# Two mixer layers on one core: the q, k, z and gm projections by Strassen's product, ahead of values and attention

## The chip, the core and the metric

The kernel runs on one core of one Trainium2 chip. The metric is the device time of one execution in microseconds (us). The kernel before took 2031.75 us, the median of 3 runs (2031.7 to 2031.75). Beside it stands the profile of one execution, taken by the hardware profiler. Its engines are PE (TensorE matmul), PEld (TensorE weight load), DVE (VectorE), ACT (ScalarE), POOL (GpSimd) and SP (SyncE, which here only issues DMAs).

## The reference, cut to what matters

Two layers run over 512 latent and 256 context tokens of 1024 features. Each layer normalises its input, projects it by one large matrix, runs two token mixers of 8 heads each (retention and mLSTM, forwards and backwards), and merges them under gates:

```
h  = rmsnorm(x) * (1 + scale) + shift                     # 768 tokens x 1024
u  = h @ w_in + b_in                                       # 1024 -> 11 * 1024 + 32
rq, rk, rv, rz, mq, mk, mv, mo, mz, mg, gr, gm = split(u)  # 1024 each, mg 32
mq, mk = silu(dwconv5(mq, mk)) ; rq, rk = rope(rq, rk) on latent tokens
rx = retention(rq, rk, rv) ; mx = mlstm(mq, mk, mv, mg)    # chunks of 128 tokens, both directions
yr = headnorm(rx) * silu(rz) ; ym = headnorm(sigmoid(mo) * mx) * silu(mz)
y  = sigmoid(gr) * (yr @ w_ret_o) + sigmoid(gm) * (ym @ w_ml_o)
x  = x + gate * (y @ w_out)
```

In the last layer only the latent tokens of the output are wanted, so context tokens need k and v alone there (`need` is false). The matrices are float32 and the result is held to float32.

## The kernel before, in words

Activations lie transposed: features on the 128 partitions, tokens on the free axis, the 256 context tokens first. h is kept as two tiles of 8 feature blocks, a float32r part (hi) and its remainder (lo). Every weight block (1024 x 128, 512 KB) is loaded from DRAM and split in the same way: `split` lets ACT write the float32r part and DVE write `raw - hi` (L161, L162). A projection of one block of 128 output features (`proj`, L208) is 8 feature blocks times three products (hi*hi, hi*lo, lo*hi): 24 matmuls over the 512 latent tokens (L216) and, where context is wanted, 24 over the 256 context tokens (L218), all summed in PSUM. Values are projected with tokens on the partitions (`projv`, L232, 256 columns a matmul).

There are 56 such blocks of q, k, z and gm in a layer: rq, rk, rz, mq, mk, mz and gm, 8 blocks each. In layer 0 all 56 need context; in layer 1 only the 16 of rk and mk do. Their results are used at once and stay on chip: rotary for rq and rk (`rope`: DVE reads the PSUM result three times, POOL adds, L651 to L654), the 5-tap convolution for mq and mk (`ml_qk`: ACT copies PSUM to u, DVE makes six passes over 770 or 512 columns, L789 to L797), silu for rz and mz (`gate_z`), and a tanh for gm, which alone goes to DRAM and comes back at the merge.

The order of the work: generators stand for the attention of a head (`ret_att`, `ml_att`) and for side work; after every projection `tick()` advances each of them by one stage, so that the matmuls of the next heads' projections stand between the attention matmuls of a head. Side work is the computation of the later modulation vectors (`ada_rest`, 32 blocks: 14 scalar_tensor_tensor passes of 128 columns and a few small ones on DVE for each block, L354 to L356; 12 blocks run in layer 0's retention stage, 20 from the gm stage on) and the mLSTM gates. A scheduler then settles each engine's instruction order. Buffers: two weight slots (`wh`, `wl`), three raw slots, six stage tiles, five large tiles of 24 KB a partition (tags b0 to b4; b0 and b1 hold h, b2 to b4 the attention's workspace).

## Time and profile before

| of the profiled execution | |
|---|---|
| span, first to last instruction | 2032.1 us (the page gives no other time of it; the runs' median is 2031.75) |
| PE busy | 1990.1 us (98%), 12676 matmuls |
| PEld busy | 1799.9 us (89%) |
| DVE busy | 1427.0 us (70%), 3303 instructions |
| ACT busy | 718.9 us (35%) |
| POOL busy | 370.0 us (18%), 431 instructions |
| granted TensorE clock, mean | 0.993 of 2.4 GHz |
| DMA | 229.59 MB, 113 GB/s |

How to read it: an engine's busy time is the time in which at least one of its instructions is under way, waiting for operands' ports included. One instruction's duration reaches some way into the next one's, so a row of instructions takes less than the sum of their durations. A stretch's limit is read from the stretch, not from these shares.

### The profile page before, as it was taken

The page shows a single profiled execution, that of the slowest core. Times are in us where ns is not written, and L with a number is a line of the kernel's source. Part 1 is how long each engine was busy: PE and PEld are TensorE (multiplying, and loading weights), DVE is VectorE, ACT ScalarE, POOL GpSimd, SP SyncE. Part 2 cuts the span into 40 slices and gives each one's busy share as a digit, 9 for nine tenths or more (in the row PEclk, how much of TensorE's full clock was granted, in tenths as well). Part 3 has the DMA queues.
Part 4 walks back from the last instruction along what each step waited for, and adds up shares of the span by engine and source line. Part 5 has one row for each costly group of instructions (what it writes and reads, how often), then busy time and mean ns, then how long its engine had stood idle before and what let it go on. Part 6 is the DMA issues. An engine that isn't in the chain of part 4 may idle for free.

```text
span 2032.1 us, 32593 instructions
## 1 busy us (share of the span) xinstructions
PE 1990.1 (98%) x12676; PEld 1799.9 (89%) x12676; DVE 1427.0 (70%) x3303; ACT 718.9 (35%) x1362; POOL 370.0 (18%) x431
## 2 busy tenths in 40 slices
PE   6989999999999999999999999999999999999997
PEld 6988989999999999888888888899899999988887
DVE  7886996566858585888834689655667886763356
ACT  5423222334434434343212442322334444434223
POOL 4312222221212121100000341312212122110000
PEclk9999999999999999999999999999999999999999
DMA  8213322212322323454524431222233333325435
GB/s 297 75 45 104 123 81 84 71 57 101 106 82 88 100 85 98 162 175 153 175 86 158 152 101 45 96 71 76 76 112 103 117 120 121 114 98 184 137 120 171
DMA packets 74716, 229.59 MB, mean 113 GB/s; under 512 B 8960, under 2 KB 17408, under 8 KB 73536
## 3 DMA queue, kind: packets, MB, share of 16 engines
q1 hardware_dynamic: 70464, 211.56, 32.0%
q0 software_dynamic: 4096, 15.93, 2.0%
q8 instruction: 100, 1.64, 0.3%
q14 instruction: 56, 0.46, 0.1%
HBM read 206.29 MB, written 21.17 MB: 112 GB/s over the span
## 4 chain that ended last, share of the span: by engine, by line
PE 87%; DVE 9%; issue 2%; DMA 1%; ACT 0%; POOL 0%; SPq 0%; POOLq 0%; DVEq 0%; ACTq 0%
PE mv L232 11%; PE mqk_l L216 9%; PE rqk_l L216 7%; PE bm_l L216 4%; PE gm_l L216 4%; PE br_l L216 4%; PE mz_l L216 4%; PE gr_l L216 4%; PE rv L232 4%; PE ou L205 4%; PE mqk_c L218 3%; PE rz_l L216 3%; PE rqk_c L218 2%; PE ro L743 2%; PE mo L869 2%
## 5 line engine op out<-in xcount | busy, mean ns | idle before, releaser
L232 PE MATMUL mv<-wh_vo,h_hi 128*128 128x256 f32 x640 | 183.6, 287 | 0.0
L232 PE MATMUL mv<-wl_vo,h_hi 128*128 128x256 f32 x640 | 183.2, 286 | 0.0
L232 PE MATMUL mv<-wh_vo,h_lo 128*128 128x256 f32 x640 | 182.0, 284 | 0.0
L356 DVE SCALAR_TENSOR_TENSOR aacc<-gw,sil,aacc 128x128 f32<-128x128 f32 x448 | 138.7, 362 | 0.0
L232 PEld LDWEIGHTS mv<-wh_vo,h_hi 128*128 128x128 f32 x640 | 122.6, 191 | 0.4
L232 PEld LDWEIGHTS mv<-wh_vo,h_lo 128*128 128x128 f32 x640 | 122.5, 191 | 0.2
L792 DVE SCALAR_TENSOR_TENSOR cv<-u,vec,cv 128x770 f32<-128x770 f32 (+1 forms) x128 | 121.3, 949 | 1.8
L232 PEld LDWEIGHTS mv<-wl_vo,h_hi 128*128 128x128 f32 x640 | 122.4, 191 | 0.0
L822 POOL TENSOR_TENSOR ws<-ws,gw 128x768 f32<-128x768 f32 (+1 forms) x32 | 53.3, 1686 | 321.5 <-PE mo L871 155.1
L216 PE MATMUL mqk_l<-h_lo,wh_mqk 128*128 128x512 f32 x256 | 103.8, 405 | 0.0
L216 PE MATMUL mqk_l<-h_hi,wh_mqk 128*128 128x512 f32 x256 | 103.3, 403 | 0.0
L216 PE MATMUL mqk_l<-h_hi,wl_mqk 128*128 128x512 f32 x256 | 102.4, 400 | 0.0
L654 POOL TENSOR_TENSOR ws<-ws,rp 128x512 f32<-128x512 f32 x32 | 52.6, 1644 | 189.6 <-DVE ws L653 149.6
L232 PE MATMUL rv<-wl_rv,h_hi 128*128 128x256 f32 x288 | 83.2, 289 | 0.0
L232 PE MATMUL rv<-wh_rv,h_hi 128*128 128x256 f32 x288 | 83.1, 289 | 0.0
L232 PE MATMUL rv<-wh_rv,h_lo 128*128 128x256 f32 x288 | 82.8, 288 | 0.0
L205 PE MATMUL ou<-yl,wh_wout 128*128 128x256 f32 (+1 forms) x256 | 79.1, 310 | 0.0
L205 PE MATMUL ou<-yh,wl_wout 128*128 128x256 f32 (+1 forms) x256 | 79.1, 310 | 0.0
L205 PE MATMUL ou<-yh,wh_wout 128*128 128x256 f32 (+1 forms) x256 | 78.7, 309 | 0.0
L743 PE MATMUL ro<-ws,ws 128*128 128x128 f32 x448 | 65.2, 279 | 9.5 <-DVE gsm L563 3.9
L695 POOL TENSOR_TENSOR ws<-ws,ws 128x768 f32<-128x768 f32 (+1 forms) x32 | 53.1, 1678 | 106.4 <-PE ro L743 106.2
L743 PEld LDWEIGHTS ro<-ws,ws 128*128 128x128 f32 x448 | 59.7, 194 | 12.8 <-DVE st L744 8.1
(444 smaller groups left out, 6536.2 us busy)
## 6 DMA issues: line engine op xcount, KB each, us to landing
gw<-in_wada SPq DMA_DIRECT2D x32, 512.0 KB, 3.4
raw_vo<-in_wblk SPq DMA_DIRECT2D x32, 512.0 KB, 4.2
raw_mqk<-in_wblk SPq DMA_DIRECT2D x32, 512.0 KB, 3.8
raw_wout<-in_wout SPq DMA_DIRECT2D x32, 512.0 KB, 3.9
gw<-grow SPq DMA_DIRECT2D x8, 1536.0 KB, 6.3
raw_qk<-in_wblk SPq DMA_DIRECT2D x16, 512.0 KB, 3.4
raw_zq<-in_wblk SPq DMA_DIRECT2D x16, 512.0 KB, 3.3
...
```

The lines of the kernel that those rows point to most:

```text
L205: pe.matmul(dst, lw[:, j, kb], mv[:, kb, sl], start=first, stop=last)
L216: pe.matmul(lat, lw[:, j, kb], mv[:, kb, LAT], start=first, stop=last)
L218: pe.matmul(c[:, :NCTX], lw[:, j, kb], mv[:, kb, CTX], start=first, stop=last)
L232: pe.matmul(dst, sx[:, kb, tk], mv[:, :, kb], start=first, stop=last)
L356: v.scalar_tensor_tensor(o, raw[:, kb], sil[:, kb, d:d + 1], o, op0=OP.mult, op1=OP.add)
L654: g.tensor_tensor(dst[:, LAT], dst[:, LAT], t[:, :512], op=OP.add)
L695: g.tensor_tensor(chunks(qd[d][:, qsl], nq), chunks(qT[:, qsl], nq), xi[d][:, None, :].to_broadcast([P, nq, P]), op=OP.mult)
L743: pe.matmul(o, lt, rt, start=k == 0, stop=k == len(ops) - 1)
L792: v.scalar_tensor_tensor(y[:, o0:o0 + n], u[:, o0 + i:o0 + i + n], cw[i], y[:, o0:o0 + n], op0=OP.mult, op1=OP.add)
L822: g.tensor_tensor(qd[d][:, qsl], qT[:, qsl], gw[:, 2 + d, qsl], op=OP.mult)
L869: pe.matmul(o, ch(sT[d], n), vt[:, n, 0:129], start=True, stop=first)
```

## The change: what it does

At the start of each layer, before any value or attention, all 56 blocks of q, k, z and gm are projected. The first four gm blocks are computed as before (`plain`). The other 52 go two at a time through Strassen's product in Winograd's form (`strassen`): the weight pair is a 2 x 2 grid of parts (two output blocks by two halves of the features), h is a 2 x 2 grid (two halves of the features by two halves of the tokens, 384 tokens each, or 256 where only latent tokens are wanted). Seven products of 12 matmuls (`product`, L684: 4 feature blocks times the three hi/lo products, 384 or 256 columns) stand in place of the eight of a plain block product.

The sums that this needs are new work. Of h, four combinations T1 to T4 are made once a layer (`make_forms`: POOL adds hi and lo, DVE makes the differences, then `split`). Of each weight pair POOL makes four sums or differences of 512 columns (`prep`, L652 to L660), and seven forms are split by ACT and DVE, 512 columns each, where two blocks of 1024 were split before. Of the products, ACT copies three partial sums out of PSUM and DVE adds three PSUM results to them (`out`, L694); `done` then does the rotary, convolution, silu or tanh from SBUF, and writes each block to DRAM from POOL's queue. Twelve blocks of `ada_rest` are ticked into this phase in layer 0. The tokens of h are stored in a permuted order, weights go through four single slots w0 to w3 and four quarter-size raw tags.

Then comes `rvg` and, in place of the old mixed loop, value projections with the attention of the heads; q, k and z of a head are fetched from DRAM two or three heads ahead (`fetch_qk`, `fetch_z`). gr is computed after the attention, its first half through DRAM. The merge and output stages are as before.

On DVE, in layer 0 before the change, the convolution of mLSTM head 0 stands between the statistics of retention head 7 and the split of the next weights (`cv` convolution, `st`, `mvs` statistics, `wl_vo` weights):

```order
L789 TENSOR_SCALAR cv_0_0_4142<-u_0_0_4141,vec_98 128x770
L792 SCALAR_TENSOR_TENSOR cv_0_0_4142<-u_0_0_4141,vec_98,cv_0_0_4142 128x770 x4
L795 SCALAR_TENSOR_TENSOR ws_0_470<-u_0_0_4141,cv_0_0_4142 128x512
L797 SCALAR_TENSOR_TENSOR ws_0_470<-u_0_0_4141,cv_0_0_4142 128x256
L744 BN_STATS st_7_4272<-ro_7_0_4273 128x6
L162 TENSOR_TENSOR wl_vo_0_4314<-raw_vo_0_0_4315,wh_vo_0_4313 128x1024
L745 BN_AGGR mvs_7_4271<-st_7_4272 128x2
L744 BN_STATS st_7_4272<-ro_7_2_4282 128x6
L162 TENSOR_TENSOR wl_vo_0_4314<-raw_vo_0_1_4319,wh_vo_0_4313 128x1024
L745 BN_AGGR mvs_7_4271<-st_7_4272 128x2
```

After the change, in the phase ahead of the attention (`w_st_11` forms of weight pair 11, `cv_mk` and `cv_mq` convolutions of two different pairs, `aacc` modulation vectors, `ub` the results; pairs count from 0):

```order
L175 TENSOR_TENSOR w_st_11_2692<-raw_st_11_01_2667,w_st_11_2692 128x512
L379 TENSOR_SCALAR aacc_12_2630<-gw_474,sil 128x128
L556 TENSOR_SCALAR cv_mk_2760<-ub_824,vec_98 128x770
L379 TENSOR_SCALAR aacc_12_2630<-gw_474,sil 128x128
L175 TENSOR_TENSOR w_st_11_2769<-raw_st_11_10_2553,w_st_11_2769 128x512
L175 TENSOR_TENSOR w_st_11_2769<-raw_st_11_11_2555,w_st_11_2769 128x512
L562 SCALAR_TENSOR_TENSOR cv_mq_2489<-ub_824,cv_mq_2489 128x770
L381 SCALAR_TENSOR_TENSOR aacc_12_2630<-gw_474,sil,aacc_12_2630 128x128
L175 TENSOR_TENSOR ahl_12_2627<-aacc_12_2417,ahl_12_2627 128x256
L559 SCALAR_TENSOR_TENSOR cv_mk_2760<-ub_824,vec_98,cv_mk_2760 128x770
L540 SCALAR_TENSOR_TENSOR ub_824<-rzt_2_2660,ub_824 128x768
```

The convolution, the silu of a z pair and the modulation vectors now stand among the splits of the weight forms, several pairs' work at once; no attention work is there.

On POOL, in the retention stage of layer 0 before (`rp` rotary adds, `ve_r` the norm's power, `yrd` results to DRAM, L695 the decayed queries):

```order
L623 TENSOR_TENSOR ve_r_3_2699<-ve_r_3_2699,nhalf 128x6
L654 TENSOR_TENSOR ws_0_470<-ws_0_470,rp_5_0_2912 128x512
L636 DMA yrd_3_480<-yo_r_3_2918 128x768
L654 TENSOR_TENSOR ws_0_470<-ws_0_470,rp_5_1_3037 128x512
L695 TENSOR_TENSOR ws_0_472<-ws_0_470,ws_0_472 128x768 x2
L623 TENSOR_TENSOR ve_r_4_3141<-ve_r_4_3141,nhalf 128x6
L675 TENSOR_TENSOR ws_0_472<-rt_5_3282 128x128
L636 DMA yrd_4_481<-yo_r_4_3270 128x768
L654 TENSOR_TENSOR ws_0_470<-ws_0_470,rp_6_0_3444 128x512
L654 TENSOR_TENSOR ws_0_470<-ws_0_470,rp_6_1_3500 128x512
```

After the change, in the new phase (`raw_st` weight sums in place, `ub` with L652 and L655 the two shared sums, `mkd`, `rkd`, `mzd` results to DRAM):

```order
L652 TENSOR_TENSOR ub_824<-raw_st_8_10_2071,raw_st_8_11_2073 128x512
L563 DMA mkd_1_527<-cv_mk_1808 128x770
L656 TENSOR_TENSOR raw_st_8_10_2071<-raw_st_8_00_2069,raw_st_8_10_2071 128x512
L563 DMA mkd_0_526<-cv_mk_1849 128x770
L549 TENSOR_TENSOR ub_824<-ub_824,rp_rk_1951 128x2x256
L550 DMA rkd_1_503<-ub_824 128x768
L660 TENSOR_TENSOR raw_st_7_01_2025<-raw_st_7_01_2025,ub_824 128x512
L655 TENSOR_TENSOR ub_824<-ub_824,raw_st_8_00_2069 128x512
L652 TENSOR_TENSOR ub_824<-raw_st_9_10_2237,raw_st_9_11_2239 128x512
L541 DMA mzd_1_535<-ub_824 128x768
L656 TENSOR_TENSOR raw_st_9_10_2237<-raw_st_9_00_2235,raw_st_9_10_2237 128x512
```

Four 512-column adds for each pair of weight blocks and the rotary adds stand in one row with the DMA issues of the results, which each wait for DVE's last pass over that result.

The diff, cut to its core:

```diff
+            def done(kind, j, u, n):
+
+                dst = st[kind][j]
...
+                elif kind in ("rz", "mz"):
+                    t = stage(f"{kind}t{l}_{j}")
+                    s.activation(t[:, :2 * n], u[:, :2 * n], AF.Tanh, scale=0.5)
+                    v.scalar_tensor_tensor(u[:, :2 * n], t[:, :2 * n], 1.0, u[:, :2 * n], op0=OP.add, op1=OP.mult)
+                    g.dma_start(dst[:, :2 * n], u[:, :2 * n])
+                elif kind in ("rq", "rk"):
...
+                    v.tensor_tensor(tv[0:64], ul[64:128], sv[64:128], op=OP.mult)
+                    v.tensor_tensor(tv[64:128], ul[0:64], sv[0:64], op=OP.mult)
+                    v.tensor_tensor(ul, ul, nat2(cosT), op=OP.mult)
+                    g.tensor_tensor(ul, ul, tv, op=OP.add)
+                    g.dma_start(dst[:, :2 * n], u[:, :2 * n])
...
+                    cw = [vc[:, V_CW + blk * 5 + i:V_CW + blk * 5 + i + 1] for i in range(5)]
+                    v.tensor_scalar(y[:, o0:o0 + m], u[:, o0:o0 + m], cw[0], vc[:, V_CB + blk:V_CB + blk + 1],
+                                    op0=OP.mult, op1=OP.add)
+                    for i in range(1, 5):
+                        v.scalar_tensor_tensor(y[:, o0:o0 + m], u[:, o0 + i:o0 + i + m], cw[i], y[:, o0:o0 + m],
+                                               op0=OP.mult, op1=OP.add)
+                    s.activation(u[:, o0:o0 + m], y[:, o0:o0 + m], AF.Tanh, scale=0.5)
+                    v.scalar_tensor_tensor(y[:, o0:o0 + m], u[:, o0:o0 + m], 1.0, y[:, o0:o0 + m], op0=OP.add, op1=OP.mult)
+                    g.dma_start(dst[:, o0:o0 + m], y[:, o0:o0 + m])
...
+            def make_forms(sl):
+                n = 256 if sl is LAT else P
+                c0 = P if sl is LAT else 0
+                for k in range(4):
+                    t0, t1 = stage(f"fa{l}_{k}_{n}"), stage(f"fb{l}_{k}_{n}")
+                    for t, kb in ((t0, k), (t1, k + 4)):
+                        g.tensor_tensor(nat2(t[:, :2 * n]), hv2(hp[0][:, kb].bitcast(F32), sl), hv2(hp[1][:, kb].bitcast(F32), sl),
+                                        op=OP.add)
+                    (a0, b0_), (a1, b1_) = [(t[:, 0:n], t[:, n:2 * n]) for t in (t0, t1)]
+                    f12, f34 = stage(f"fc{l}_{k}_{n}"), stage(f"fd{l}_{k}_{n}")
+                    v.tensor_tensor(f12[:, 0:n], b0_, a0, op=OP.subtract)
+                    v.tensor_tensor(f12[:, n:2 * n], b1_, f12[:, 0:n], op=OP.subtract)
+                    v.tensor_tensor(f34[:, 0:n], b1_, b0_, op=OP.subtract)
+                    v.tensor_tensor(f34[:, n:2 * n], a1, f12[:, n:2 * n], op=OP.subtract)
+                    for f, tf in ((f12, t12), (f34, t34)):
+                        split(tf[:, 0, :, k, c0:c0 + n], tf[:, 1, :, k, c0:c0 + n], nat2(f[:, :2 * n]))
...
+            def strassen(pairs):
+
...
+                def prep(i, k):
+                    if i >= nu:
+                        return
+                    w = wslot(k, f"st{l}_{i}")[:, :2 * KB * P].rearrange("p (f h c) -> p f h c", f=2, h=2)
+                    W[i, k] = w
+                    r = R[i]
+
+                    def form(f, a):
+                        split(w[:, f, 0], w[:, f, 1], a)
+                    if k == 0:
+                        g.tensor_tensor(s1b, r[1, 0], r[1, 1], op=OP.add)
+                        form(0, r[0, 0])
+                        form(1, s1b)
+                        g.tensor_tensor(s2b, s1b, r[0, 0], op=OP.subtract)
+                        g.tensor_tensor(r[1, 0], r[0, 0], r[1, 0], op=OP.subtract)
+                    elif k == 1:
+                        form(0, s2b)
+                        form(1, r[0, 1])
+                        g.tensor_tensor(r[0, 1], r[0, 1], s2b, op=OP.subtract)
+                    elif k == 2:
+                        form(0, r[1, 0])
+                        form(1, r[1, 1])
+                    else:
+                        form(0, r[0, 1])
...
+                def product(i, ps, k, f, form, first, last):
+                    n = pairs[i][2]
+                    w = W[i, k]
+                    for kk in range(4):
+                        xh, xl = act(form, kk, n)
+                        for hl, x in ((0, xh), (0, xl), (1, xh)):
+                            pe.matmul(ps[:, :n], w[:, f, hl, kk * P:(kk + 1) * P], x, start=first and kk == 0 and hl == 0 and x is xh,
+                                      stop=kk == 3 and hl == 1, skip_group_check=True)
+
+                def out(i, o, half, ps, add=None):
+                    kind, j0, n = pairs[i]
+                    b = vc[:, VB[kind] + j0 + o:VB[kind] + j0 + o + 1]
+                    for dst, c in pieces(kind, U[i][o], half, n):
+                        if add is None:
+                            s.activation(dst, ps[:, c], AF.Identity, bias=b)
+                        else:
+                            v.scalar_tensor_tensor(dst, ps[:, c], b, add[:, c], op0=OP.add, op1=OP.add)
...
+                three = (("ra", 0, 0), ("rb", 1, 0), ("rc", 1, 1))
+                raws_of(0, three + (("rd", 0, 1),))
+                prep(0, 0)
+                prep(0, 1)
+                yield
+                for i, (kind, j0, n) in enumerate(pairs):
+                    U[i] = [ub[:, 774 * (2 * (i % 2) + o):774 * (2 * (i % 2) + o + 1)] for o in range(2)]
+                    u2s = ub[:, 3864 + 384 * (i % 2):4248 + 384 * (i % 2)]
+                    if kind in ("mq", "mk"):
+                        for u in U[i]:
+                            pads(u, n)
+                    raws_of(i + 1, three)
+                    X[i], Z[i] = atile("lat", f"sx{l}_{i}"), atile("ctx", f"sz{l}_{i}")
+                    product(i, X[i], 0, 0, "B11", True, False)
+                    s.activation(p1s[:, :n], X[i][:, :n], AF.Copy)
+                    product(i, Z[i], 0, 1, "T1", True, False)
+                    yield
+                    p4(i - 1)
+                    prep(i, 2)
+                    product(i, X[i], 1, 0, "T2", False, False)
+                    s.activation(u2s[:, :n], X[i][:, :n], AF.Copy)
+                    yield
+                    p3(i - 1)
+                    prep(i, 3)
+                    raws_of(i + 1, (("rd", 0, 1),))
+                    prep(i + 1, 0)
+                    Y = btile(f"sy{l}_{i}")
+                    product(i, Y, 1, 1, "B21", True, True)
+                    out(i, 0, 0, Y, p1s)
+                    prep(i + 1, 1)
+                    product(i, X[i], 2, 0, "T3", False, False)
+                    s.activation(u3s[:, :n], X[i][:, :n], AF.Copy)
+                    out(i, 1, 1, Z[i], u3s)
+                    yield
+                p4(nu - 1)
+                wload(wpos[0])
+                p3(nu - 1)
...
+            first = plain(0, True)
+            next(first)
+            t12 = big.tile([P, 2, 2, 4, 384], F32R, tag="b3", name=f"t12_{l}")
+            t34 = big.tile([P, 2, 2, 4, 384], F32R, tag="b4", name=f"t34_{l}")
+            make_forms(LAT)
+            for _ in first:
+                pass
+            ub = big.tile([P, 6144], F32, tag="b2", name=f"ub{l}")
+            todo = [("gm", 4, need), ("gm", 6, need)]
+            for j in (0, 2, 4, 6):
+                todo += [("mq", j, need), ("rz", j, need), ("mk", j, True), ("rk", j, True), ("mz", j, need), ("rq", j, need)]
+            run = strassen([(k, j, 384 if full else 256) for k, j, full in todo])
+            for _ in plain(2, False):
+                make_forms(CTX)
+                next(run)
+            if l == 0:
+                ada_todo = [(0, b) for b in range(16, 24)] + [(1, b) for b in range(24)]
+                side.append(ada_rest(gw, ada_todo[:ADAN]))
+            for i, _ in enumerate(run):
+                if i % 4 == 3:
+                    tick()
+            drain(side)
+
 
```

## Rows read from the trace of the kernel before

**Rows 1.** Stretches: length, sum, busy PE, PEld, DVE, ACT, POOL; PEclk, DMA share, GB/s.

```profile
100.00:150.00 50.00, 44.25 (x284) 40.87 (x283) 45.24 (x95) 10.92 (x18) 7.36 (x7) 0.93 0.14 45
220.00:310.00 90.00, 89.41 (x607) 81.93 (x606) 89.36 (x279) 28.27 (x59) 19.79 (x14) 1.00 0.30 99
570.00:675.00 105.00, 105.00 (x744) 98.12 (x743) 77.51 (x196) 42.21 (x94) 20.39 (x30) 1.00 0.29 93
```

**Rows 2.** The chain that ended last, by engine, from the page.

```profile
PE 87%; DVE 9%; issue 2%; DMA 1%; ACT 0%; POOL 0%; SPq 0%; POOLq 0%; DVEq 0%; ACTq 0%
```

**Rows 3.** Timeline of PE, three places: start us, duration us, what.

```profile
700.10 0.40 PE L216 MATMUL mqk_l<-h_hi,wh_mqk 128*128 128x512 f32 x1
...
700.45 0.40 PE L216 MATMUL mqk_l<-h_lo,wh_mqk 128*128 128x512 f32 x1
...
707.94 0.28 PE L232 MATMUL mv<-wh_vo,h_lo 128*128 128x256 f32 x1
708.06 0.28 PE L232 MATMUL mv<-wl_vo,h_hi 128*128 128x256 f32 x1
...
1850.12 0.39 PE L216 MATMUL gr_l<-h_lo,wh_gr 128*128 128x512 f32 x1
1850.35 0.39 PE L216 MATMUL gr_l<-h_hi,wl_gr 128*128 128x512 f32 x1
```

**Rows 4.** DVE groups by line and shape: busy us, mean ns, idle before.

```profile
L356 DVE SCALAR_TENSOR_TENSOR aacc<-gw,sil,aacc 128x128 f32<-128x128 f32 x448 | 138.7, 362 | 0.0
L792 DVE SCALAR_TENSOR_TENSOR cv<-u,vec,cv 128x770 f32<-128x770 f32 x96 | 97.5, 1016 | 1.4
...
L162 DVE TENSOR_TENSOR wl_mqk<-raw_mqk,wh_mqk 128x1024 fp32r<-128x1024 f32 x32 | 38.5, 1219 | 12.7 <-ACT wh_mqk L161 12.7
...
L792 DVE SCALAR_TENSOR_TENSOR cv<-u,vec,cv 128x512 f32<-128x512 f32 x32 | 23.9, 746 | 0.3
...
L1082 DVE SCALAR_TENSOR_TENSOR X<-ou,mod,X 128x256 f32<-128x256 f32 x24 | 11.4, 479 | 16.8 <-PE ou L205 11.4 <-DMA X<-x1d 5.4
...
L611 DVE SCALAR_TENSOR_TENSOR ws<-mzt,ws 128x768 f32<-128x768 f32 x8 | 7.6, 954 | 3.0 <-ACT ws L610 3.0
...
L1082 DVE SCALAR_TENSOR_TENSOR X<-ou,mod,X 128x512 f32<-128x512 f32 x8 | 6.0, 751 | 19.5 <-PE ou L205 19.5
...
L162 DVE TENSOR_TENSOR yl<-G,yh 128x512 fp32r<-128x512 f32 x8 | 5.5, 688 | 2.9 <-ACT yh L161 2.9
```

**Rows 5.** Timeline of DVE at two places.

```profile
576.37 0.85 DVE L812 TENSOR_SCALAR ws<-ws,gcol 128x129 f32<-128x129 f32 x3 [0.48 <-PE mkv L833]
577.14 0.99 DVE L838 SCALAR_TENSOR_TENSOR ws<-ws,gdec,mkv 128x129 f32<-128x129 f32 x3
...
592.60 0.68 DVE L789 TENSOR_SCALAR cv<-u,vec 128x770 f32<-128x770 f32 x1 [4.74 <-ACT u L786]
```

**Rows 6.** Timeline of POOL from 1154 us, between the layers.

```profile
1154.57 3.54 POOL L386 TENSOR_TENSOR xn<-X,rst 128x512 f32<-128x512 f32 x2 [3.25 <-DMA x1d<-X]
1158.07 1.59 POOL L366 TENSOR_TENSOR sq<-X 128x256 f32<-128x256 f32 x1
1159.63 1.29 POOL L386 TENSOR_TENSOR xn<-X,rst 128x512 f32<-128x512 f32 x1
```

**Rows 7.** Timeline of DVE in the same stretch.

```profile
1155.48 3.72 DVE L162 TENSOR_TENSOR wl_wout<-raw_wout,wh_wout 128x1024 fp32r<-128x1024 f32 x2 [0.50 <-ACT wh_wout L161]
1159.12 0.47 DVE L1082 SCALAR_TENSOR_TENSOR X<-ou,mod,X 128x256 f32<-128x256 f32 x1
1159.70 1.50 DVE L368 TENSOR_TENSOR acc<-acc,sq 128x256 f32<-128x256 f32 x1
1161.13 2.39 DVE L162 TENSOR_TENSOR h_lo<-xn,h_hi 128x512 fp32r<-128x512 f32 x2
```

**Rows 8.** POOL groups of the norms' power and of result DMAs' issues.

```profile
L623 POOL TENSOR_TENSOR ve_m<-ve_m,nhalf 128x6 f32<-128x6 f32 (+1 forms) x16 | 20.7, 1294 | 64.4 <-DVE ve_m L622 64.3
...
L636 POOL DMA_DIRECT2D yrd<-yo_r x16 | 10.0, 627 | 68.4 <-DVE yo_r L634 64.3 <-DVE aacc L356 3.9 <-issue 0.2
```

More of the change, by code (lines that the diff above doesn't have):

```diff
@@ L38 @@
 BORD = [1, 0, 5, 4, 3, 2]
+POS = [0, 3, 1, 2, 4, 5]
+KO = [0, 4, 1, 5, 2, 6, 3, 7]
 CTX = slice(0, NCTX)
@@ L408, in pair @@
                 spec(f"{name}_{l}", wb[l, a], wb[l, b])
+            for j in (0, 2):
+                pair(f"gm{j}", B_GM + j, B_GM + j + 1)
             for p in range(4):
@@ L459, in start_ctx @@
             rstd_rows(acc, rst, CTX, "ms_inc")
-            for kb in range(KB):
-                modulate(0, xin, rst, hp, CTX, kb)
-                if kb % 3 == 2:
-                    yield
+            yield from modulate_ctx(0, xin, rst, hp)
         main.append(start_ctx())
@@ L748, in ret_att @@
                 norm(mvs, srcs, 1.0, f"r{l}_{h}")
+                finished.add(("w", l, h))
                 yield
@@ L905, in build @@
                     vt = chunks(vts[0][:, :1536])
-                    def rvg(n):
+                    for n in range(NCH):
                         ps = projvg(wv, hp, n, f"rvg{l}_{n}")
@@ L1060, in after @@
                 rstd_rows(acc, rst, sl, f"ms{l}_{sl.start}")
-                for kb in range(KB):
+                for i, kb in enumerate(KO if need else range(KB)):
                     if need:
```

408 lines of the change are left out of this document (227 added, 181 removed).

## The prediction

> **What bounds the kernel now.** I read the busy shares by stretch first. With projections and attention mixed, PE works through the whole stretch: 105.00 of 105.00 us in the mLSTM heads with DVE at 77.51, 89.41 of 90 in the retention heads with DVE at 89.36 [rows 1]. The chain of waits agrees: 87% PE, 9% DVE [rows 2]. So matmul time removed there is worth its full length, but only while DVE follows: in the retention heads DVE is already as full as PE. POOL looks idle (19.79 of 90), and the next steps turn on what that idleness is worth. The sums are made against the profiled span, 2032.1 us, 0.35 above the median of the runs, a difference I neglect.
>
> **PE, removed and added.** Starts show what a matmul costs in a row: a 512 and a 256 together 0.35 to 0.36 us (700.10 to 700.45), a 256 alone 0.12, a 512 alone 0.23 [rows 3]. No 384 stands in the trace; bounds from the same rows are 0.12 and 0.23, and I take 0.355 x 384/768 = 0.178. Removed: in layer 0, 56 blocks x 24 x 0.355 = 477 us; in layer 1, 16 x 24 x 0.355 + 40 x 24 x 0.227 = 354 us; together 831. Added: a pair has 7 products of 12 matmuls. Layer 0: 26 x 84 x 0.178 = 389, and four plain gm blocks 4 x 24 x 0.347 = 33, so 422. Layer 1: 18 x 84 x 0.12 + 8 x 84 x 0.178 + 4 x 24 x 0.227 = 323. Together 745. If PE stayed the bound, the change would win 831 - 745 = 86 us. If a 384 cost 0.23, layer 0 would need 114 more and all of that would be gone.
>
> **DVE in the new phases.** Prices are the groups' means [rows 4] less the 0.08 us by which an instruction reaches into the next (576.37 + 0.85 = 577.22 against a start at 577.14) [rows 5]. A split of 512 is 0.61 (where two of 1024, 2 x 1.14, served two blocks, seven of 512 now serve a pair); a convolution pass of 770 is 0.94, its first 0.60 [rows 5], so a block with six passes 5.3; z 0.87; a PSUM reader of 256 0.40, of 512 0.67, so one of 384 0.54 between them; a modulation block 14 x 0.28 and some small passes, 5.2. A rotary pass I price as a split.
> Layer 0, a round of six pairs: 42 splits 25.6; PSUM adds 12 x 0.54 + 6 x 0.67 (the convolution pairs write two pieces, 256 and 128) = 10.5; four convolutions 21.2; four z blocks 3.5; twelve rotary passes 7.3; sum 68.1, times four 272. Two gm pairs 12, the forms of h 16, the plain gm weights 5, twelve modulation blocks 62: 367 us, 45 of it reading PSUM. Layer 1, where most blocks have 512 tokens: the convolution of 512 costs 0.67 a pass, so a round is 61.8; 4 x 61.8 + 11 + 16 + 5 = 279, 36 of it reading PSUM. Alone, DVE would fit under PE in both layers (367 under 422, 279 under 323).
>
> **POOL, and what its sums cost DVE.** An addition of 512 takes 1.29 alone [rows 6], 1.25 in a row. A layer's 26 pairs need 104, the rotary 16, the forms eight of 512 and eight of half that: 150 + 16 = 166 us. That is far below PE's time, but where POOL adds SBUF operands, DVE's SBUF passes stand still. Between the layers two POOL products of 512 and two DVE splits of 1024 run from 1154.57 to 1159.20, 4.63 us [rows 6, 7]; one after the other they would take 2 x 1.25 + 2 x 1.14 = 4.78. So 97% of the sum remains, hardly any overlap. In the same rows two DVE splits of 512 take 2.39 instead of 1.30, and an accumulation of 256 takes 1.50 beside POOL's 1159.63; but the passage that reads PSUM, 1159.12, takes 0.47 inside POOL's 1158.07 to 1159.66, as its group does alone (0.479).
> The Trainium skill, page "SBUF — State Buffer", section "Who interferes with whom", states this as a lock: a DVE instruction that needs both its ports and a GpSimd instruction exclude each other for the whole of an instruction, and one with a single SBUF operand goes free. The trace agrees (2.39 against 0.47). By the rule alone the phases would take the whole of that sum, 488 and 409 us, and the time would be 2032 + 66 + 10 = 2108.
> Bounds of the phases: no exclusion at all leaves PE, 422 and 323; full turn-taking leaves 367 + 166 = 533 and 279 + 166 = 445. By the nearest rows (97% of the sum, PSUM readers left out) it is 0.97 x (367 - 45 + 166) = 473 and 0.97 x (279 - 36 + 166) = 397. I take 485 and 405, a little above, because POOL runs its queue in order: a result's DMA (0.63 us to issue [rows 8], 52 a layer after the first blocks) waits there for DVE's last pass over that result, and behind it stand the next pair's additions, for which ACT, DVE and PE wait; and because PE's seven products a pair must end before DVE's three PSUM adds. Removed 831, added 485 + 405 = 890: +59 us.
>
> **What is moved out of the attention.** Its matmuls stay; of DVE's work there the convolutions, z, rotary and part of the weight splits go. What goes with them is cover: until now a head's waits lay behind projections. The stretch of 105 us in the mLSTM is two heads long [rows 1]. PE loses six blocks (two each of q, k, z), 6 x 24 x 0.355 = 51, and keeps (105 - 51)/2 = 27 us a head. DVE loses four convolutions 21.2, two z 1.7 and six weight splits 6.8, and keeps (77.5 - 29.7)/2 = 23.9. PE stays the longer, so I expect most waits to stay hidden. Upper bound: the POOL power in the norm of a head, 1.29 us [rows 8], stands open in each of 32 heads, 41 us. Lower bound: the retention heads lose DVE's overload and PE gets back what it waited, 0.6 of 90 us [rows 1], some 3 us over the stage. I take +10, the wait open in one head of four, since in the mixed stretch PE never stopped. Stores and fetches add 112 blocks x 0.39 MB each way, 88 MB on 230, beside a DMA share of 0.3 [rows 1]: hidden; if the fetches' lead of two heads failed, a fetch at the stretch's 93 GB/s would be 4.2 us a block.
> Sum: 2032 + 59 + 10 = 2101, **2100 us**.
>
> **Rivals.**
> Faster, PE stays the bound: POOL's sums are hidden under PE because the scheduler lays them beside PSUM readers and ACT's steps. Time: 2032 - 86 + 10 = 1956. It decides if a pair's turn-taking stays under PE's 15 us in layer 0 and 10 in layer 1. For it: DVE can run at 89.36 of 90 while PE is full [rows 1], and POOL is 18% busy. Against: the work of both engines on SBUF alone is 473 and 397 by rows, over PE's 422 and 323. Chance 0.16.
> Break-even: the lower bounds hold, and the modulation blocks, which have low priority, slide into the value stage, so that layer 0 gives up 62 and PE sets its 422; with layer 1 at 397 that is 819 in place of 831, and with +10 the time is 2030. For it: layer 0 without them needs 0.97 x (322 - 62 + 166) = 413. Against: they are ticked into the phase at a fixed rate and hold shared tiles. Chance 0.12.
> Attention exposed: with no projections between, each head waits for its own normalisation chain, the POOL power (1.29) [rows 8] and two passes around it of 0.61, 2.5 us for each of 32 heads, 80 us in place of 10: 2171. For it: 9% of the chain is DVE [rows 2]. Against: PE is still the longer by the head's sum. Chance 0.12.
> Clock: PE waits in the new phases by (485 - 422)/26 = 2.4 us a pair in layer 0 and (405 - 323)/26 = 3.2 in layer 1. In the stretch where PE waited, 44.25 of 50 busy, the granted clock was 0.93 of 2.4 GHz, so part of it ran at 1.2 and 0.07 x 50 = 3.5 us of PE's time were lost [rows 1]. If each pair's waits in layer 1 bring half such a drop, 26 x 1.75 = 45: 2145. Against: DVE sets that phase, and a slower PE is mostly hidden under it. Chance 0.06.
>
> **How the numbers follow.** The forecast has 0.54; its own range is 2050 to 2150, from the lower bounds without exposed attention (2032 + 39, less 20 for partly sliding modulation blocks) to the full sums with nothing hidden (2032 + 147 + 10 = 2189, drawn in to 2150 because PSUM readers were seen to overlap). What a measurement can tell from no change is 0.2%, about 4 us. Slower by more than that: the forecast 0.54, exposed attention and clock 0.18, and 0.02 of the break-even, 0.74; faster: the first rival 0.16 and half of the break-even, 0.22; within: the other 0.04. The range goes from 1985, which takes in part of the first rival (some turns taken, PE nearly the bound) to 2175, leaving out its full win and the worst exposed attention.
>
> **What would show it.** Right: POOL near 700 us busy and DVE near 100% through both new phases, about 485 and 405 us long; weight splits of 512 well above 0.69 us on average because they wait for POOL; PE's idle time there released by DVE's splits; PE nearly full from the values on. Wrong: PE full in the new phases and splits at 0.69 (then 1956), phases as forecast but PE idle in the heads (then the attention's term is too small), or a 384 matmul with a spacing of 0.23.

## The result and the profile after

The changed kernel takes 2369.26 us (median of 4 runs, 2360.86 to 2370.48) against 2031.72 us (4 runs, 2031.45 to 2031.75): ratio 1.1653, interval 1.1635 to 1.1671. Slower, as forecast, but by 337 us and not by 69: the time lies far outside the range. The profiled execution has a span of 2359.0 us, 327 more than before.

First the busy times of the page, then the same execution cut at the places where the work changes: the projection phase of layer 0, its values, attention and gr, the merge and output, and the same for layer 1; the last five rows are parts of the phases. The columns are the stretch's bounds, its length, busy time (instructions) of PE, PEld, DVE, ACT and POOL, granted clock, DMA share and GB/s.

```profile
PE 2047.6 (87%) x12916; PEld 1901.3 (81%) x12916; DVE 1847.8 (78%) x3977; ACT 876.1 (37%) x1876; POOL 772.5 (33%) x779
```

```profile
core 0: us, PE busy (x) PEld busy (x) DVE busy (x) ACT busy (x) POOL busy (x), PEclk, DMA share, GB/s
32.60:579.90 547.30, 469.25 (x2490) 441.46 (x2489) 498.39 (x801) 212.95 (x403) 258.66 (x260) 0.93 0.32 108
579.90:1105.50 525.60, 469.80 (x3370) 442.62 (x3369) 378.65 (x1164) 182.49 (x473) 137.91 (x126) 0.94 0.41 132
1105.50:1317.20 211.70, 207.39 (x1199) 182.05 (x1198) 169.10 (x465) 67.94 (x118) 12.10 (x9) 1.00 0.53 174
1317.20:1751.00 433.80, 352.76 (x2219) 330.08 (x2217) 401.45 (x501) 183.77 (x363) 238.21 (x241) 0.91 0.30 101
1751.00:2212.50 461.50, 394.58 (x2755) 368.17 (x2756) 293.01 (x860) 158.30 (x396) 111.46 (x131) 0.93 0.41 130
2212.50:2359.00 146.50, 136.01 (x785) 120.15 (x783) 82.94 (x150) 50.92 (x97) 1.78 (x2) 0.97 0.46 150
70.00:130.00 60.00, 34.96 (x154) 29.59 (x155) 48.84 (x71) 19.65 (x38) 40.76 (x40) 0.67 0.11 36
1345.00:1400.00 55.00, 25.77 (x144) 22.21 (x143) 54.16 (x71) 20.54 (x42) 39.81 (x37) 0.66 0.13 44
230.00:330.00 100.00, 83.39 (x433) 77.98 (x431) 99.57 (x173) 36.46 (x67) 41.47 (x47) 0.95 0.35 119
32.60:172.60 140.00, 110.66 (x583) 99.13 (x582) 100.85 (x174) 53.99 (x105) 76.08 (x74) 0.84 0.29 101
1317.20:1357.20 40.00, 27.07 (x131) 21.59 (x129) 30.49 (x43) 16.25 (x28) 22.76 (x26) 0.91 0.23 79
```

Before, the same work (the projections and the attention mixed) took two stretches, of layer 0 and of layer 1:

```profile
35.60:961.10 925.50, 918.15 (x6169) 842.82 (x6169) 705.22 (x1857) 327.28 (x689) 185.61 (x208) 1.00 0.31 101
1165.80:1885.90 720.10, 711.33 (x4420) 638.10 (x4419) 495.76 (x1053) 264.97 (x505) 154.19 (x198) 1.00 0.32 103
```

So 925.5 became 547.3 + 525.6 = 1072.9, and 720.1 became 433.8 + 461.5 = 895.3; of the rest, the merge of layer 0 took 7 us more and the start 3 less. Three things are to be seen. In the middle of a projection phase (230 to 330) DVE is full, 99.57 of 100, and PE waits. Early in each phase (70 to 130 and 1345 to 1400, where the first pairs start) PE works for half of the time, at a clock of 0.67 and 0.66. And in the attention no engine is full: PE 470 of 526 and 395 of 462, where PE never stopped in the mixed stretch before [rows 1], and the clock is 0.94 and 0.93 in place of 1.00. By the clock records TensorE was at 1.2 GHz for 299 us of the span, 208 of them while busy, so half of that, 104 us, is work done at half speed (before: 17 busy, 8.5 lost). PE's idle time rose from 42 to 311 us. 269 + 95 - 38 (PE's own work is less) = 326, the difference of the spans.

The turn-taking of [rows 6, 7] is in the phase itself. The groups of DVE and of POOL (busy us, mean ns, idle before), and a stretch of both engines (start, duration):

```profile
L175 DVE TENSOR_TENSOR w_st<-raw_st,w_st 128x512 fp32r<-128x512 f32 x260 | 215.6, 841 | 34.3 <-ACT w_st L174 33.5
L381 DVE SCALAR_TENSOR_TENSOR aacc<-gw,sil,aacc 128x128 f32<-128x128 f32 x448 | 166.7, 418 | 0.1
L175 DVE TENSOR_TENSOR w_st<-ub,w_st 128x512 fp32r<-128x512 f32 x104 | 102.6, 988 | 4.0 <-ACT w_st L174 3.8
...
L694 DVE SCALAR_TENSOR_TENSOR ub<-sz,vec,ub 128x384 f32<-128x384 f32 x44 | 26.9, 610 | 3.1 <-ACT ub L743 2.6 <-PE sz L684 0.2
```

```profile
L660 POOL TENSOR_TENSOR raw_st<-raw_st,ub 128x512 f32<-128x512 f32 x52 | 83.8, 1611 | 80.8 <-DVE w_st L175 80.8
L652 POOL TENSOR_TENSOR ub<-raw_st,raw_st 128x512 f32<-128x512 f32 x52 | 81.1, 1560 | 144.3 <-DMA raw_st<-in_wblk 108.1 <-DVE w_st L175 15.8 <-DVE ub L694 7.5
```

```profile
248.73 2.26 POOL L660 TENSOR_TENSOR raw_st<-raw_st,ub 128x512 f32<-128x512 f32 x1 [2.91 <-DVE w_st L175]
251.07 1.29 POOL L655 TENSOR_TENSOR ub<-ub,raw_st 128x512 f32<-128x512 f32 x1
```

```profile
247.96 1.88 DVE L175 TENSOR_TENSOR w_st<-raw_st,w_st 128x512 fp32r<-128x512 f32 x3
249.96 0.62 DVE L694 SCALAR_TENSOR_TENSOR ub<-sz,vec,ub 128x384 f32<-128x384 f32 x1
...
251.11 1.81 DVE L546 TENSOR_TENSOR rp_rk<-ub,gw 64x512 f32<-64x512 f32 x1
252.93 0.69 DVE L547 TENSOR_TENSOR rp_rk<-ub,gw 64x512 f32<-64x512 f32 x1
```

Here each engine waits for the other: POOL's 248.73 takes 2.26 in place of 1.29 while DVE ends its three splits; DVE's rotary pass at 251.11 takes 1.81 beside POOL's 251.07, where the next one of its size, 252.93, takes 0.69; the reader of PSUM at 249.96 keeps its 0.62 inside POOL's addition. A split that was 0.688 alone [rows 4] is 0.841 and 0.988 on average, the PSUM reader of 384 stays at 0.610 (I had 0.54 + 0.08). The matmul of 384 columns has a spacing of 0.173 us (0.178 forecast).

In the attention, what PE waited for in layer 0 (us in total, times, longest), and in the last line the largest entry of layer 1:

```profile
PE yt_r L928 <- ACT ws L921: 14.0, 4, 4.8
PE mkv L1092 <- DVE ws L1097: 11.7, 6, 4.6
PE yt_m L928 <- ACT ws L921: 7.8, 1, 7.8
PE mo L1128 <- DVE ws L1097: 6.2, 7, 1.8
PE ro L1024 <- DVE st L1025: 4.5, 5, 2.6
...
PE rk L912 <- DMA ws<-rkd: 2.6, 1, 2.6
...
PE yt_r L928 <- ACT ws L921: 16.5, 4, 6.8
```

These are few and long waits inside the heads' own chains: the transposes of the output (yt) for the normalisation, the chunk products (mkv, mo) for the states' steps. A fetch from DRAM (rkd) held PE once, for 2.6 us. One of the waits on PE's timeline, with the windows around it:

```profile
798.50 1.70 PE L990 MATMUL rkv<-ws,ws 128*128 128x256 f32 x8 [0.51 <-DVE ws L972]
805.00 1.17 PE L928 MATMUL yt_r<-k_ident,ws 128*128 128x128 f32 x3 [4.80 <-ACT ws L921]
805.96 1.06 PE L1024 MATMUL ro<-ws,ws 128*128 128x128 f32 x4
```

```profile
800.20:805.00 4.80, 0.00 (x1) 0.00 (x1) 4.12 (x14) 0.89 (x4) 2.62 (x2) 0.90 0.28 82
805.00:812.00 7.00, 7.00 (x37) 6.67 (x37) 3.85 (x11) 2.88 (x8) 0.82 (x3) 0.58 0.21 48
```

PE stands for 4.8 us at a transpose, and in the 7 us behind, though it is busy throughout, the clock is 0.58: most of it at 1.2 GHz. The wait is paid a second time.

### The profile page after: what moved, and what is told of

Same layout as the page of the kernel before. It is cut to its first block, busy times and chain, and to the rows that moved or that the text cites. A ratio compares the mean times of both kernels' runs of the same rounds, so it can differ in the third digit from the quotient of the medians.

```text
span 2359.0 us, 36311 instructions
## 1 busy us (share of the span) xinstructions
PE 2047.6 (87%) x12916; PEld 1901.3 (81%) x12916; DVE 1847.8 (78%) x3977; ACT 876.1 (37%) x1876; POOL 772.5 (33%) x779
## 5 line engine op out<-in xcount | busy, mean ns | idle before, releaser
L684 PE MATMUL sx<-t,w_st 128*128 128x384 f32 (+1 forms) x1872 | 337.3, 328 | 52.7 <-DVE w_st L175 32.2
L684 PEld LDWEIGHTS sx<-t,w_st 128*128 128x128 f32 x1872 | 305.6, 197 | 68.1 <-DVE w_st L175 40.7
L258 PE MATMUL mv<-w_vo,h_hi 128*128 128x256 f32 x1280 | 256.6, 295 | 15.5 <-DVE ws L1043 11.1
L175 DVE TENSOR_TENSOR w_st<-raw_st,w_st 128x512 fp32r<-128x512 f32 x260 | 215.6, 841 | 34.3 <-ACT w_st L174 33.5
L258 PEld LDWEIGHTS mv<-w_vo,h_hi 128*128 128x128 f32 x1280 | 208.5, 196 | 20.2 <-DVE ws L1043 8.1
L174 ACT ACTIVATE w_st<-raw_st 128x512 fp32r<-128x512 f32 x260 | 155.9, 625 | 168.8 <-DMA raw_st<-in_wblk 91.0
L258 PE MATMUL mv<-w_vo,h_lo 128*128 128x256 f32 x640 | 187.3, 293 | 0.0
L684 PE MATMUL sz<-t,w_st 128*128 128x384 f32 (+1 forms) x624 | 115.8, 332 | 30.7 <-ACT w_st L174 12.7
L684 PE MATMUL sz<-h_hi,w_st 128*128 128x384 f32 (+1 forms) x416 | 115.2, 346 | 24.4 <-DVE ub L694 24.1
L684 PEld LDWEIGHTS sz<-t,w_st 128*128 128x128 f32 x624 | 103.7, 200 | 36.1 <-ACT w_st L174 12.9
L652 POOL TENSOR_TENSOR ub<-raw_st,raw_st 128x512 f32<-128x512 f32 x52 | 81.1, 1560 | 144.3 <-DMA raw_st<-in_wblk 108.1
L258 PEld LDWEIGHTS mv<-w_vo,h_lo 128*128 128x128 f32 x640 | 125.8, 197 | 0.4
L684 PE MATMUL sy<-h_hi,w_st 128*128 128x384 f32 (+1 forms) x416 | 110.0, 330 | 15.5 <-ACT w_st L174 9.7
L684 PE MATMUL sx<-h_hi,w_st 128*128 128x384 f32 (+1 forms) x416 | 112.9, 333 | 6.5 <-ACT ub L692 3.5
L660 POOL TENSOR_TENSOR raw_st<-raw_st,ub 128x512 f32<-128x512 f32 x52 | 83.8, 1611 | 80.8 <-DVE w_st L175 80.8
L684 PEld LDWEIGHTS sz<-h_hi,w_st 128*128 128x128 f32 x416 | 80.9, 208 | 29.6 <-DVE ub L694 29.6
```

Source lines behind the costliest of these rows:

```text
L174: s.activation(dh, src, AF.Copy)
L175: (eng or v).tensor_tensor(dl, src, dh.bitcast(F32), op=OP.subtract)
L258: pe.matmul(dst, sx[:, kb, tk], mv[:, :, kb], start=first, stop=last)
L652: g.tensor_tensor(s1b, r[1, 0], r[1, 1], op=OP.add)
L660: g.tensor_tensor(r[0, 1], r[0, 1], s2b, op=OP.subtract)
L684: pe.matmul(ps[:, :n], w[:, f, hl, kk * P:(kk + 1) * P], x, start=first and kk == 0 and hl == 0 and x is xh, stop=kk == 3 and hl == 1, ski ...
```

## The experiments

All times are medians, with the kernel before at 2031 to 2033 us in the same sets of runs; intervals of the ratios are 0.002 to either side. The stretches are cut as above, from the profiled executions.

| kernel | us | ratio | phase 0 | attention 0 | phase 1 | attention 1 |
|---|---|---|---|---|---|---|
| changed kernel | 2369.3 | 1.165 | 547 | 526 | 434 | 462 |
| sums_on_dve | 2310.7 | 1.138 | 525 | 530 | 393 | 471 |
| no_sums | 2215.1 | 1.091 | 478 | 522 | 358 | 459 |
| plain_phase | 2230.5 | 1.098 | 508 | 520 | 358 | 450 |
| gr_cover | 2350.5 | 1.158 | 551 | 508 | 435 | 459 |
| yt_later | 2326.0 | 1.145 | 551 | 500 | 436 | 454 |
| ticks_spread | 2360.2 | 1.162 | 551 | 518 | 434 | 463 |
| fill | 2382.8 | 1.172 | 548 | 530 | 433 | 473 |
| ada_later | 2354.8 | 1.159 | 497 | 525 | 433 | 461 |
| no_pow | 2319.2 | 1.141 | 549 | 504 | 435 | 439 |
| yt_later2 | 2294.9 | 1.129 | 548 | 492 | 428 | 434 |
| ynb2_later2 | 2279.7 | 1.121 | 551 | 477 | 432 | 428 |
| ynb2_later4 | 2237.5 | 1.101 | 551 | 472 | 432 | 392 |
| no_forms | 2344.4 | 1.152 | 537 | 524 | 420 | 467 |
| strassen_best | 2245.0 | 1.105 | 507 | 503 | 381 | 460 |
| plain_best | 2182.6 | 1.074 | 506 | 488 | 359 | 431 |
| plain_ynb2 | 2105.1 | 1.036 | 506 | 452 | 359 | 394 |

**The phases: POOL's sums.** In `prep`, the four sums by DVE:

```diff
-                        g.tensor_tensor(s1b, r[1, 0], r[1, 1], op=OP.add)
+                        v.tensor_tensor(s1b, r[1, 0], r[1, 1], op=OP.add)
...
-                        g.tensor_tensor(r[0, 1], r[0, 1], s2b, op=OP.subtract)
+                        v.tensor_tensor(r[0, 1], r[0, 1], s2b, op=OP.subtract)
```

> The four sums of each weight pair are made by DVE instead of POOL; nothing else changes. Turn-taking (POOL's additions keep DVE's passes over SBUF waiting, so what counts is the sum of both): 104 x 1.25 = 130 us of POOL leave each phase, 104 x 0.61 = 63 come to DVE, so each phase can shrink by up to 67 us; PE's own 447 and 380 us stop it sooner in layer 0, so about 45 and 55: 2270 us (2235 to 2300), although DVE, the fuller engine, gets more work. Rival, DVE is bound by its own passes and POOL's sums lie free beside them: DVE's list grows by 63 us a layer, 2495 us. Rival, the phase is a chain of latencies (sum, split, product, copy, add): each sum is shorter by 0.6 us, about the same, 2340 to 2370 us.

Measured 59 us less; the time is 11 us above the range that I expected. The two phases of that kernel, and the splits in it:

```profile
32.50:557.50 525.00, 451.86 (x2468) 430.47 (x2467) 469.53 (x901) 214.11 (x402) 99.85 (x153) 0.93 0.34 111
1299.00:1691.70 392.70, 340.93 (x2219) 323.68 (x2217) 369.76 (x599) 186.28 (x360) 96.04 (x137) 0.92 0.33 109
```

```profile
L175 DVE TENSOR_TENSOR w_st<-raw_st,w_st 128x512 fp32r<-128x512 f32 x260 | 179.8, 702 | 21.6 <-ACT w_st L174 21.2
L175 DVE TENSOR_TENSOR w_st<-ub,w_st 128x512 fp32r<-128x512 f32 x104 | 73.3, 707 | 0.6 <-ACT w_st L174 0.6
```

The first pass of the convolution, in the changed kernel and in this one:

```profile
L556 DVE TENSOR_SCALAR cv_mk<-ub,vec 128x770 f32<-128x770 f32 x16 | 20.5, 1286 | 0.0
L556 DVE TENSOR_SCALAR cv_mk<-ub,vec 128x770 f32<-128x770 f32 x16 | 10.8, 688 | 0.3 <-issue 0.3
```

DVE got 104 instructions more a layer and was busy for less time (498 to 470, 401 to 370), because its splits no longer wait: 841 to 702 ns, 988 to 707. Of DVE's busy time in the changed kernel a good part was waiting for POOL. The rival that POOL's sums are free is out. The size was less than I expected: 22 of 45 us in layer 0 and 41 of 55 in layer 1, and the attention took 4 and 9 us more.

Without the sums (the calls are deleted, `form` reads the raw parts):

```diff
-                        g.tensor_tensor(s1b, r[1, 0], r[1, 1], op=OP.add)
...
-                        form(1, s1b)
+                        form(1, r[1, 1])
```

> The four sums of each weight pair are left out; the seven forms are split from the raw parts as they are, so the number of splits, products and outputs is unchanged. Turn-taking: the phases fall to about what PE needs with its first waits, 523 to about 455 us and 461 to about 390 us: 2230 us (2200 to 2260). Rival, POOL's sums are hidden: no change, 2360 to 2375 us. If it comes out within 20 us of the kernel with the sums on DVE, PE is the limit of both.

Measured 154 us less, and phases of 478 and 358:

```profile
32.60:510.50 477.90, 443.46 (x2490) 429.07 (x2489) 413.01 (x803) 216.01 (x407) 97.52 (x156) 0.96 0.38 124
1244.00:1602.30 358.30, 328.46 (x2233) 316.19 (x2232) 314.07 (x502) 186.53 (x365) 85.39 (x139) 0.96 0.38 122
```

So the sums, with all that waits for them, cost 69 and 76 us. The kernel comes out 96 below the one with the sums on DVE, more than the 20 us that I had set as the mark for PE as the limit of both: with the sums on DVE, PE isn't the limit, and DVE is still the fuller engine (470 of 525 and 370 of 393 us).

**The order without the product.** The pairs go through the old product, in the same phase and with the same DRAM trip; `make_forms` and `strassen` are gone:

```diff
-            run = strassen([(k, j, 384 if full else 256) for k, j, full in todo])
+            run = plain_pairs([(k, j, 384 if full else 256) for k, j, full in todo])
...
+                        for ps, sl in proj(w, o, hp, n == 384, f"{kind}{l}_{j0 + o}"):
...
+                        done(kind, j0 + o, u, n)
```

> The phase ahead of values and attention stays, with its DRAM round trip, but the 26 pairs are projected by the plain product (2 x 24 matmuls of 512 and, with context, of 256 columns), without forms of h and without weight sums. Lost cover (the attention waits for its own chains because no projection stands between): values and attention take 512 and 448 us as in the changed kernel, the phases fall to PE's 477 + about 25 and 354 + about 20: 2369 - 23 - 86 = 2260 us (2220 to 2290). Rival, the attention is slow from what the Strassen phase leaves behind (DVE and POOL backlog, late results): it goes back to about 422 and 362 us as before, 2085 us.

```profile
32.70:540.30 507.60, 497.41 (x2839) 434.82 (x2838) 299.22 (x589) 165.99 (x308) 77.64 (x143) 0.98 0.39 128
540.30:1060.50 520.20, 465.26 (x3335) 438.37 (x3334) 368.40 (x1140) 179.49 (x467) 134.25 (x123) 0.94 0.38 122
1277.30:1635.20 357.90, 352.03 (x1730) 295.52 (x1729) 210.34 (x303) 136.28 (x241) 66.58 (x126) 1.00 0.42 136
1635.20:2085.10 449.90, 386.32 (x2693) 359.26 (x2692) 283.28 (x841) 153.91 (x383) 106.37 (x125) 0.93 0.39 122
```

This divides the loss: 199 us belong to the order (2230 against 2031), 139 to the product. The attention takes 520 and 450 us as with Strassen's product (526 and 462), so what Strassen's phase leaves behind is worth 6 and 12 us there at most. The phases are PE's here (497 of 508, 352 of 358). Strassen's product makes them 40 and 76 us longer, though it takes 28 us off PE in layer 0 even at the lower clock (469 against 497). Even without the weight sums (no_sums) its phases are 478 and 358 beside the 508 and 358 of the plain product: it is ahead by 30 us in layer 0 and by nothing in layer 1.

**The attention: cover or distance.** Two gr pairs of a layer moved between the heads (weights in that order, results through DRAM):

```diff
+            gr_early(0)
             gate_rows(0)
...
+                if h == 4:
+                    gr_early(1)
```

> Four of the eight gr blocks of each layer (8.5 us of PE each in layer 0, 5.4 in layer 1) move from behind the attention into it: two between retention and mLSTM, two after the values of mLSTM head 4; through DRAM, as half of them went already. Lost cover: part of 34 + 22 us goes under waits of PE, about 30 to 40 us less, 2330 us (2310 to 2345). Rival, the waits are in the heads' own chains and other work at two places doesn't fill them, or the first half of gr was cover where it stood: 2362 to 2380 us.

Measured 19 us less, between the two expectations: 18 in layer 0's attention and 3 in layer 1's. Matmuls at two places cover little. Advancing the stages in smaller steps (`projv` ticks inside):

```diff
+                    if 8 * i + kb + 1 in at:
+                        tick(False)
```

> The attention's stages are advanced inside a value projection (after 15, 33 and 48 of its 48 matmuls in retention, 24 and 48 in mLSTM) and no longer two or three at once behind it; all work is the same. If the cover was lost because stages now follow one another with no matmuls between them: 20 to 60 us less, 2325 us. Rival, it is the amount of cover per head that is missing, or the scheduler already lays the value matmuls between the stages: 2355 to 2380 us.

Measured 9 us less, the rival. Then the transposes one stage later:

```diff
                 yield
                 yield
+                yield
                 head_out(
```

> In every head the transposes of the normalised output (yt) are issued one stage of the interleaving later; all work is the same. Theory of the heads' own chains: PE stands in its fixed order at yt while ACT's normalisation of that head is late, 46 us in the changed kernel, with lower clock behind each wait; one stage later most of it is covered: 2320 us (2300 to 2340). Rival, the heads hang on one another through the single workspace (ynb, hsb, qd, sT), so that a later yt only delays the next head: 2360 to 2390 us.

Measured 43 us less (of the medians; the profiled executions, of which the changed kernel's is its fastest, differ by 30: 26 and 8 less in the two attentions, some 4 more elsewhere). Two stages:

> The output transposes come two stages later than in the changed kernel (one stage gave 43 us). If more distance is what the chains lack: 2300 to 2320 us. If the single buffers between heads then bind (the next head's normalisation waits until ynb has been read): 2325 to 2360 us, nothing more gained than with one stage.

Measured 74 us less, more than expected. In this one the next head overwrites ynb, the normalised output, before the transposes have read it, so they work on another head's data; the time tells what distance gives, the single buffer what forbids it. The step of the chain that stands on POOL was left out instead:

```diff
-                g.tensor_tensor(ve[:, 1, :nq], ve[:, 0, :nq], nhalf.to_broadcast([P, nq]), op=OP.pow)
```

> The power of the headnorm (POOL, 1.3 us a head) is left out, the rest of the chain stays. The prediction's upper bound had this power open in each of 32 heads, 41 us: 2328 us. The theory that PE waits for whole chains only where its fixed order comes too early (10 long waits before yt in the changed kernel, 43 us together): 10 x 1.3 us and some clock, 2350 us (2335 to 2360). Rival, the power is hidden: 2365 to 2372 us.

Measured 50 us less, more than either number: 1.6 us a head on average over 32 heads, with the clock that came back. Ten steps of 1.3 us are 13, so more hangs on this chain than the ten long waits; how the gain is spread over the heads is not shown. With a second ynb (in place of the third z buffer) the distance is free to grow:

```diff
-            ynb = ws3[:, 5376:6144]
+            ynbs = [ws3[:, 5376:6144], ws1[:, 4608:5376]]
...
-            zTs = [ws1[:, 3072 + 768 * i:3840 + 768 * i] for i in range(3)]
+            zTs = [ws1[:, 3072 + 768 * i:3840 + 768 * i] for i in range(2)]
```

> A second buffer for the normalised output (ynb, in the place of the third z buffer; z is fetched two heads ahead instead of three), and the output transposes two stages later than in the changed kernel. Single workspace and distance: as with one stage (2326) and some 25 to 35 us more, 2297 us (2280 to 2312). If the distance has nothing more to give: 2320 to 2330 us.

> The same with four stages. If PE's fixed order met the chains too early, all waits before yt go and those behind the states' steps are left (some 35 us a layer idle, and their clock): 2270 us (2255 to 2295). If the amount of matmuls beside a head is what is missing, the distance runs out: no faster than with two stages, 2290 to 2310 us.

Measured 2279.7 and 2237.5, both better than expected: 132 us of the loss came back, with the same matmuls and the same cover. The attention with four stages:

```profile
583.50:1055.20 471.70, 446.23 (x3370) 426.83 (x3370) 376.84 (x1171) 182.81 (x476) 136.24 (x126) 0.98 0.46 149
1697.10:2088.80 391.70, 372.73 (x2755) 353.46 (x2756) 291.80 (x863) 156.77 (x397) 111.33 (x131) 0.98 0.50 155
```

PE idles 25 and 19 us here (56 and 67 in the changed kernel) and the clock went up to 0.98 with it.

**The clock.** Matmuls that nobody reads, before the waits:

```diff
+                for k in range(4):
+                    pe.matmul(ps, hp[0][:, 0, 0:P], hp[0][:, k, 0:512], start=True, stop=True)
```

> 64 groups of four matmuls of 512 columns, whose result nobody reads, are put before waits in the attention (before each head's output transposes and before the last chunk products): 58 us of PE at full clock. If PE's clock, which falls to 1.2 GHz behind the waits, costs the attention some 50 us beside the waits themselves, the fillers lie in the 123 us of idle and keep the clock up: 2330 to 2370 us, no slower in spite of more work. Rival, the fillers stand where PE has work, or the clock doesn't follow them: 2390 to 2430 us.

```profile
580.30:1110.30 530.00, 489.69 (x3499) 456.86 (x3498) 377.68 (x1153) 182.39 (x472) 137.61 (x126) 0.97 0.41 131
1761.60:2235.00 473.40, 415.92 (x2882) 383.02 (x2883) 290.75 (x862) 158.64 (x395) 112.16 (x131) 0.96 0.40 126
```

Between the two expectations: 58 us of added work cost 14 us. The clock rose from 0.94 and 0.93 to 0.97 and 0.96 and the idle time fell from 123 to 98, so the clock does follow the waits; filling them with useless work doesn't pay.

**What else fills the phases.** The modulation blocks moved out (`ADAN = 0`):

> The twelve modulation blocks leave layer 0's projection phase and are made after the attention with the other twenty. If DVE and POOL together set that phase, it loses up to 62 us of its 547, down to PE's 440 to 470 with its waits; the stages behind have room for most (DVE 169 of 212 us there and 100 of 130 beside gr), +15: 2325 us (2305 to 2345). Rival, the phase's waits are its chain's and not DVE's load: 2365 to 2385 us.

Measured 14 us less, between the two expectations. Layer 0's phase fell by 50 us as expected, to 497, and layer 1's stayed at 433. But between the layers, where the changed kernel's PE goes over without a stop, there are now 38 us with PE busy for 8.5:

```profile
1270.20:1308.00 37.80, 8.46 (x28) 5.89 (x26) 25.96 (x93) 10.25 (x20) 4.53 (x5) 0.57 0.28 88
```

PE waits there for the last modulation blocks (16.8 us at `ada` for ACT) and for the sums of layer 1's norm, which DVE makes (6.4 us). The forms of h left out (parts of h are split in their place):

> The forms of h are not computed: POOL's 16 sums and DVE's 32 differences a layer are left out, the splits stay, so that T1 to T4 are just parts of h. If the forms hold up the start of the phases, where PE idles 25 and 29 us and runs at 1.2 GHz for another 35 and 13: 15 to 25 us less in each layer, 2330 us (2315 to 2345). Rival, the start waits for h and the first weights in any case: 2355 to 2372 us.

25 us less, 11 and 14 in the phases. The forms explain a part of the slow starts and not the whole.

**Together.** All that helped, with Strassen's product and without:

> All that helped, with Strassen's product kept: the weight sums, the sums of the forms and the rotary's addition by DVE, and the output transposes one stage later. Turn-taking and chains as two separate causes, so that their gains add up: 2369 - 59 - 43 - about 20 = 2247 us (2225 to 2275). If they are one and the same loss: 2290 to 2310 us. Either way above the kernel before.

> The order of the change without Strassen's product, with all that helped: transposes one stage later, four gr blocks inside the attention, the rotary's addition by DVE: 2230 - 43 - 19 = 2168 us (2145 to 2190). What is left over 2032 is the price of the order that these edits can't mend. If it came under 2060, the order would cost nothing once the stages are set for it.

> The order of the change without Strassen's product, with the second ynb, transposes three stages later, four gr blocks inside the attention and the rotary's addition by DVE. With distance: 2183 (one stage) less 30 to 50, 2142 us (2125 to 2160). What stays over 2032 is then waits at the other places of a head's chain; under 2060 the order would be free.

Measured 2245.0, 2182.6 and 2105.1. The first of them is what the sum of the gains gave, so turn-taking and chains are two causes; 20 us of that sum, for the forms' sums and the rotary on DVE, had not been measured alone. With three stages and the second ynb the order without the product is 3.6% slower than before (interval 3.4 to 3.8), and lower than my 2142. No version beat the kernel before, and none of these results points to one: in the kernel before, PE is busy for 918 of 925 and 711 of 720 us, and in the edited phases Strassen's product (507 and 381) is no shorter than the plain one (506 and 359).

## Why the prediction was wrong

- **That turn-taking makes the phases longer than the projections they replace: right.** DVE is full in the middle of the phase, its splits wait for POOL, and the sums cost 69 and 76 us. The rival in which PE stays the bound is out. The Trainium skill's "SBUF — State Buffer", section "Who interferes with whom", says that the loser waits for a whole instruction and that a DVE instruction with at most one SBUF input, outside DVE's two-port modes, does not contend; the rows at 248.73 and 249.96 agree (2.26 against 1.29, and 0.62 unchanged). The prediction left that exception out, and not every pass with one SBUF input went free: the convolution's first pass, a tensor_scalar, took 1.286 us beside POOL's sums and 0.688 without them. In which mode it ran no run shows.
- **PE's matmul time: the price right, the saving too high.** A matmul of 384 came every 0.173 us. But PE's own work, the clock taken out, fell by 38 us and not by 86: it is 441 and 329 in the phases (422 and 323 forecast) and 446 and 370 in the attention (438 and 354 should have stayed). The last matmul before a stop counts with its whole record, some 0.16 us longer than its spacing, and PE stops 233 times in place of 23: by estimate 34 of the missing 48 us.
- **The phases' length, 485 and 405: too low by 62 and 29 us.** DVE's busy time came near the sum, 498 and 401. But the sum took DVE as full from the first to the last instruction, and DVE stood for 49 and 32 us. In layer 0, 39 of them lie in the first 140 us (32.6 to 172.6); in layer 1, 10 lie in the first 40 (1317.2 to 1357.2) and the rest is spread. At the start the first pairs wait for h, the forms, the sums and the splits one after another, and PE has little else to do (35 of 60 and 26 of 55 us busy). No term stood for that. In layer 0 the cut between phase and attention is rough: before, the start's waits held value projections, now they hold gm blocks.
- **"PE stays the longer, so I expect most waits to stay hidden": the step that failed.** It gave 10 us; the stretches took 526 and 462 us against 453 and 371 (what is left of before, plus 5 each), 163 us more and the largest part of the error. I compared the busy sums of a head, 27 us of PE and 23.9 of DVE, and a head isn't a sum: it is a chain over PE, DVE, ACT and POOL. Before, a mixed stage put a whole projection block, 8.5 us in layer 0, between two stages of a chain; after, the stages follow each other more closely than the chain's steps take, and PE, in its fixed order, stands at the early matmul though others are ready behind it. plain_phase shows that the order does it without Strassen's product (520 and 450), and ynb2_later4 that more distance with the same work takes 132 us of the loss back, 124 of them in the two attentions of the profiled executions. The trip through DRAM, which is part of the order, held PE itself for only 2.6 us; whether late fetches lengthen the chains on other engines no run separates.
- **Attention exposed, the rival at 2171, was the nearer case, but its 80 us are less than half of the 173 that came.** It priced the normalisation alone, 2.5 us a head; no_pow shows that this chain indeed counts (1.6 us a head on average for one step of 1.3), but the states' steps wait too, and waits are paid again in clock.
- **The clock, a rival of 45 us with chance 0.06: should have been a term beside any waiting.** 104 us of PE's time went there, some 53 in the phases and 49 in the attention. I had argued that DVE hides it; in the attention nothing does.
- **What stays open:** how much of the phases' clock loss is hidden under DVE, and what else besides the forms slows their start.
